# The low halves of a product's weights: GpSimd's subtraction tied by a semaphore to VectorE's row sums, and made two steps ahead

## The chip, the cores and the metric

The kernel runs on one core of a Trainium2 chip. The metric is the device time of one execution in microseconds (us); the profile is of one such execution on that core. Engine names are those of the profile: PE is TensorE (PEld its weight loads), DVE is VectorE, ACT is ScalarE, POOL is GpSimd, SP is SyncE, whose queue issues most loads.

## The reference, cut to what matters

Two transformer blocks run one after the other on 256 tokens of width 2048. The change lies in the last part of the second one, a layer of 16384 experts of which each token picks 128 (8 heads, 16 each):

```python
def peer_ffn(h, w_pq, sub_keys, u_tab, v_tab):
    ...
    expert = (e1 * N_KEYS + e2).reshape(T, PEER_HEADS * PEER_TOPK)
    gate = jax.nn.softmax(best, axis=-1).reshape(T, PEER_HEADS * PEER_TOPK).astype(h.dtype)
    def chunk(args):
        hc, ec, gc = args
        u = jnp.take(u_tab, ec, axis=0)
        act = jax.nn.gelu(jnp.einsum('cd,ckd->ck', hc, u), approximate=False) * gc
        vv = jnp.take(v_tab, ec, axis=0)
        return jnp.einsum('ck,ckd->cd', act, vv)
```

Its output is, for each token, a sum over its 128 picks of an activation times a row of `v_tab` (2048 wide).

## The kernel before, in words

Products are made in fp32r: a float32 operand is split into a high part (a copy rounded to fp32r) and a low part (the operand less its high part), and three matmuls (high by high, high by low, low by high) make one product.

The change lies in the second half of `_peer`, the output stage. Its result for 2 x 128 tokens lies in eight PSUM tiles `o` of 128x512: four column groups `g` for each token half `t`. The stage makes them in two ways:

- **By products, columns 0 to 1535.** The activations of all tokens for all 16384 experts lie in SBUF as `S_`, 128 slices of 128x256 (`sa` holds the first 52, `sb` the rest), zero where a token has not picked an expert. Step `e` of the loop at line 1582 multiplies slice `e` by 128 rows of `v`. It splits the slice into `ah` (ACT, line 1586) and `al` (POOL, line 1587), streams 1536 columns of `v` in three groups of 512 through `_stream`, and for each group issues, for both token halves, the matmuls (`ah`,`vh`), (`ah`,`vl`), (`al`,`vh`): 18 matmuls of 512 columns a step. The `v2` pool holds three `ah` and three `al`.
- **By rows, columns 1536 to 2047.** `_row_sums` fetches, for each of the 128 picks of every token, one row of 640 floats from the table `wide` in DRAM (512 columns of `v`, and the token's inner products with the expert). Row `j` takes two indirect DMAs from POOL's queue (line 1454), one a token half; ten row tiles `vrow` let them run four rows ahead. On DVE, one multiply a half (line 1468, a 128x128 product with the identity, summed along the row into the weight `w`) and one sum a half (line 1475: `o` plus row times weight, with `o` in PSUM) follow.

`_stream` (line 231) issues the loads of `v` on SP's queue: 1024 columns into a tile of `k.raw` (three of them) and 512 into a tile of `k.raw2` (six). For each 512 columns ACT copies `hi` (line 251) and DVE subtracts `lo` (line 254); there are four `hi` and four `lo`. In the trace these stand as `hi` and `lo` (`vh` and `vl` in the loop's words), and the matmuls as `o<-hi,ah`, `o<-lo,ah`, `o<-hi,al`, all at line 259.

The order on each engine is made by a scheduler that takes the program's order as priority. Line 1469 and line 1476 put each row's multiplies and sums behind the last `lo` on DVE, without a semaphore. The while loop at line 1598 takes one row in most steps and two in six of them, beginning at step 3.

Of the kernel before, what the change touches and what calls it, by code (L numbers as in the profile page):

```python
# [10 lines left out]
F32 = mybir.dt.float32  # L11
# [3 lines left out]
AF = mybir.ActivationFunctionType  # L15
OP = mybir.AluOpType
AX = mybir.AxisListType
NOSYNC = mybir.DependencyInfo(mybir.DependencyClass.NoSync, mybir.DependencyReason.DATA)

D = 2048  # L20
# [193 lines left out]
def _after(k, b, a):  # L214
    k.tc.add_manual_dep(b.ins, a.ins.name, NOSYNC, reason="one start per bank")

# [14 lines left out]
def _stream(k, src, total):  # L231
    nc = k.nc
    for r in range(0, total, k.rk * 256):
        n = min(total - r, k.rk * 256)
        if k.raw2 is not None and n <= 512:
            raw = k.raw2.tile([128, 512], F32, name="raw")
        else:
            raw = k.raw.tile([128, k.rk * 256], F32, name="raw")
        small = k.n == 0
        if not small:  # L240
            load = nc.sync.dma_start(raw[:, :n], src[:, r:r + n])
            if k.side:
                _after(k, nc.sync.dma_start(*k.side.pop(0)), load)
        step = 512 if small else k.gr
        for a in range(0, n, step):
            m = min(step, n - a)
            if small:
                nc.sync.dma_start(raw[:, a:a + m], src[:, r + a:r + a + m])
            hi = k.hi.tile([128, k.gr], F32R, name="hi")
            lo = k.lo.tile([128, k.gr], F32R, name="lo")  # L250
            nc.scalar.activation(hi[:, :m], raw[:, a:a + m], AF.Copy)  # L251
            k.n += 1
            eng = nc.gpsimd if k.pool_lo and k.n % k.pool_lo == 0 else nc.vector
            k.low = eng.tensor_tensor(lo[:, :m], raw[:, a:a + m], hi[:, :m].bitcast(F32), op=OP.subtract)  # L254
            yield hi, lo, m
# [96 lines left out]
def _first_mixer(k, I, rstd_n, rstd_b, mh, ml):  # L352
    nc, tc = k.nc, k.tc
    with ExitStack() as c:
# [207 lines left out]
        for pr in range(4):  # L562
# [9 lines left out]
            for hh in range(2):  # L572
# [4 lines left out]
                for t in range(2):  # L577
# [6 lines left out]
                    mx = at2.tile([128, 1], F32, name="mx")  # L584
                    nc.vector.tensor_reduce(mx, lg[:, :n], axis=AX.X, op=OP.max, negate=True)
                    sm = at2.tile([128, 1], F32, name="sm")
# [194 lines left out]
def _rwkv(k, I, rn, rb, y, qkv):  # L781
# [249 lines left out]
    def inverse(p, lq):  # L1031
# [5 lines left out]
        for t in range(1, 16):  # L1037
            nc.vector.tensor_tensor(tmp[:, :, 0:t], tt[:, :, 0:t], lq[:, 0:t, t][:, None, :].to_broadcast([128, 8, t]), op=OP.mult)  # L1038
            nc.vector.tensor_reduce(tt[:, :, t], tmp[:, :, 0:t + 1], axis=AX.X, op=OP.add)
        s2 = dram.tile([2, 4, 2, 4, 16, 16], F32, name="s2")  # L1040
# [64 lines left out]
    def chain(p, ars, pcs, am, dt, bon, gg, vz, bk):  # L1105
# [60 lines left out]
        mn = b2.tile([128, 4], F32, name="gm")  # L1166
        nc.vector.tensor_reduce(mn, y4, axis=AX.X, op=OP.add)
        nc.vector.tensor_scalar(mn, mn, 1.0 / 64, None, op0=OP.mult)
# [3 lines left out]
        vr = b2.tile([128, 4], F32, name="gv")  # L1172
        nc.vector.tensor_reduce(vr, sq2, axis=AX.X, op=OP.add)
        nc.vector.tensor_scalar(vr, vr, 1.0 / 64, 64e-5, op0=OP.mult, op1=OP.add)
# [60 lines left out]
def _gqa(k, y, qkv, g2, banks):  # L1235
# [17 lines left out]
    for m in range(8):  # L1253
# [11 lines left out]
        for h in range(2):  # L1265
# [9 lines left out]
            mx = g2.tile([128, 2], F32, name="gmx")  # L1275
            nc.vector.tensor_reduce(mx, sc, axis=AX.X, op=OP.max, negate=True)
            nc.vector.tensor_scalar(mx, mx, 0.125, None, op0=OP.mult)
# [51 lines left out]
class _Route:  # L1329
# [42 lines left out]
    def _pick(self, h, s):  # L1372
# [16 lines left out]
        for n in range(2):  # L1389
# [8 lines left out]
            for t in range(2):  # L1398
                nc.vector.tensor_tensor(eq[:, t], cf[:, t][:, :, None].to_broadcast([128, 16, 16]),
                                        self.iota[:, None, :].to_broadcast([128, 16, 16]), op=OP.is_equal)  # L1400
                nc.vector.tensor_tensor(eq[:, t], eq[:, t], fi[:, t, n][:, None, :].to_broadcast([128, 16, 16]), op=OP.mult)
            nc.vector.tensor_reduce(self.e[n][:, :, hs], eq, axis=AX.X, op=OP.add)

# [41 lines left out]
def _row_sums(k, picks, wide, rows, acc):  # L1445


    nc = k.nc
    ready = []

    def fetch(j):
        for t in range(2):
            r = rows.tile([128, DS + 128], F32, name="vrow")
            nc.gpsimd.indirect_dma_start(r, None, wide, bass.IndirectOffsetOnAxis(ap=picks.row[:, t, j:j + 1], axis=0),  # L1454
                                         element_offset=128 * t)
            ready.append(r)

    ahead = RB // 2 - 1
    for j in range(ahead):
        fetch(j)  # L1460
    for j in range(128):
        got = []
        for t in range(2):
            r = ready.pop(0)
            p, v = (r[:, DS:], r[:, :DS]) if t else (r[:, :128], r[:, 128:])

            w = picks.val[:, t, j:j + 1]
            i = nc.vector.scalar_tensor_tensor(p, p, picks.gate[:, t, j:j + 1], k.ident, op0=OP.mult, op1=OP.mult, accum_out=w)  # L1468
            _after(k, i, k.low)
            got.append((v, w))  # L1470
        for t, (v, w) in enumerate(got):
            if j == 0:
                i = nc.vector.tensor_scalar(acc[t], v, w, None, op0=OP.mult)
            else:
                i = nc.vector.scalar_tensor_tensor(acc[t], v, w, acc[t], op0=OP.mult, op1=OP.add)  # L1475
            _after(k, i, k.low)
        if j + ahead < 128:
            fetch(j + ahead)
        yield


def _peer(k, I, O, hctx, pers, sa, tctx, t1, x3n, wide, rb):
    nc, tc = k.nc, k.tc
# [20 lines left out]
    with ExitStack() as sctx:  # L1504
# [68 lines left out]

        with ExitStack() as c:
            pso = c.enter_context(tc.tile_pool(name="pso", bufs=1, space=bass.MemoryType.PSUM))
            v2 = c.enter_context(tc.tile_pool(name="v2", bufs=3, side="right"))
            k.raw2 = c.enter_context(tc.tile_pool(name="raw2", bufs=6, side="right"))
            out = [[pso.tile([128, 512], F32, name=f"o{t}{q}") for q in range(4)] for t in range(2)]
            rows = c.enter_context(tc.tile_pool(name="vr", bufs=RB, side="right"))
            sums = _row_sums(k, picks, wide, rows, [out[t][3] for t in range(2)])  # L1580
            taken = 0
            for e in range(128):
                src = S_[0][:, e] if e < SA else S_[1][:, e - SA]
                ah = v2.tile([128, 256], F32R, name="ah")
                al = v2.tile([128, 256], F32R, name="al")
                nc.scalar.activation(ah, src, AF.Copy)
                nc.gpsimd.tensor_tensor(al, src, ah.bitcast(F32), op=OP.subtract)  # L1587
                for g, (vh, vl, _) in enumerate(_stream(k, I["v"][e], D - DS)):
                    for t in range(2):
                        ts = slice(t * 128, t * 128 + 128)  # L1590
                        for n, (s_, m_) in enumerate(((ah, vh), (ah, vl), (al, vh))):
                            _mm(k, out[t][g], s_[:, ts], m_, start=e == 0 and n == 0, stop=e == 127 and n == 2)
                if e == 24:

                    xn = [S_[0][:, 8 * t:8 * t + 8].rearrange("p a b -> p (a b)").rearrange("p (a b) -> p a b", b=512) for t in range(2)]
                    for t in range(2):
                        nc.scalar.dma_start(xn[t], x3n[t].rearrange("p (a b) -> p a b", b=512))
                while taken < 128 and taken * 122 < (e - 2) * 128:
                    next(sums, None)
                    taken += 1  # L1600
            for _ in sums:
                pass
            k.raw2 = None
            sctx.close()
            fin = c.enter_context(tc.tile_pool(name="fin", bufs=1))
            nf = fin.tile([128, 4, 512], F32, name="nf")
            nc.scalar.dma_start(nf.rearrange("p a b -> p (a b)"), I["normf"].to_broadcast([128, D]))
            for t in range(2):
                ss = fin.tile([128, 4], F32, name=f"ss{t}")
                sq = fin.tile([128, 512], F32, name=f"fsq{t}")  # L1610
                for q in range(4):
                    nc.vector.tensor_tensor(xn[t][:, q], xn[t][:, q], out[t][q], op=OP.add)
                    nc.scalar.activation(sq, xn[t][:, q], AF.Square, accum_out=ss[:, q:q + 1])
                v = fin.tile([128, 1], F32, name=f"fv{t}")
                nc.vector.tensor_reduce(v, ss, axis=AX.X, op=OP.add)
                nc.vector.tensor_scalar(v, v, 1.0 / D, EPS, op0=OP.mult, op1=OP.add)
                r = _rsqrt(k, fin, v, 1, f"f{t}")
                for q in range(4):
                    nc.vector.scalar_tensor_tensor(xn[t][:, q], xn[t][:, q], r, nf[:, q], op0=OP.mult, op1=OP.mult)
                    (nc.sync if q % 2 else nc.scalar).dma_start(O["out"][t * 128:t * 128 + 128, q * 512:q * 512 + 512], xn[t][:, q])  # L1620
# [146 lines left out]
```

## Time and profile before

| | |
|---|---|
| median of 3 runs | 3388.03 us (3386.93 to 3388.34) |
| the profiled execution | 3391.95 us, its span 3390.1 us |
| PE busy over the span | 97% |
| DVE / ACT / POOL busy | 76% / 46% / 26% |
| mean granted clock of PE | 0.983 |
| HBM traffic over the span | 209 GB/s |

The page divides the span into 40 slices; the output stage fills the last seven, where DVE's digits are 9, PEld's 7 (against 9 before) and the DMA engines' 9. PE's busy time counts matmuls that overlap in the pipeline, so that a row of them with small pauses still reads as busy. How fast PE goes is read from the starts of its matmuls.

### The profile page before, as it was taken

The page shows a single profiled execution, that of the slowest core. Times are in us where ns is not written, and L with a number is a line of the kernel's source. Part 1 is how long each engine was busy: PE and PEld are TensorE (multiplying, and loading weights), DVE is VectorE, ACT ScalarE, POOL GpSimd, SP SyncE. Part 2 cuts the span into 40 slices and gives each one's busy share as a digit, 9 for nine tenths or more (in the row PEclk, how much of TensorE's full clock was granted, in tenths as well). Part 3 has the DMA queues.
Part 4 walks back from the last instruction along what each step waited for, and adds up shares of the span by engine and source line. Part 5 has one row for each costly group of instructions (what it writes and reads, how often), then busy time and mean ns, then how long its engine had stood idle before and what let it go on. Part 6 is the DMA issues. An engine that isn't in the chain of part 4 may idle for free.

```text
span 3390.1 us, 65776 instructions
## 1 busy us (share of the span) xinstructions
PE 3272.4 (97%) x25018; PEld 3050.2 (90%) x25018; DVE 2571.7 (76%) x5477; ACT 1572.2 (46%) x2810; POOL 866.4 (26%) x1036
## 2 busy tenths in 40 slices
PE   8999899999999979999999999999999999999998
PEld 8999899999999979888879999999999996777776
DVE  8775587777744468788865778776777869999999
ACT  5444444444433345555454544444444444444444
POOL 3110210000000055454410000001223226666663
PEclk9999999999999979999989999999999999999999
DMA  5545455555555568653126566666566679999996
GB/s 194 168 156 174 131 168 186 178 184 187 182 180 186 172 248 286 194 169 100 52 81 200 181 200 195 190 200 188 179 176 183 180 218 335 316 320 324 317 324 225
DMA packets 239341, 680.46 MB, mean 201 GB/s; under 512 B 58160, under 2 KB 88752, under 8 KB 214832
## 3 DMA queue, kind: packets, MB, share of 16 engines
q1 hardware_dynamic: 167824, 560.53, 51.0%
q0 software_dynamic: 20480, 83.90, 7.5%
q10 hardware_dynamic: 50720, 31.82, 3.2%
q8 instruction: 196, 3.21, 0.4%
q14 instruction: 121, 0.99, 0.1%
HBM read 649.55 MB, written 60.16 MB: 209 GB/s over the span
## 4 chain that ended last, share of the span: by engine, by line
PE 71%; DVE 17%; DMA 7%; issue 3%; ACT 1%; POOL 1%; SPq 0%; DVEq 0%; ACTq 0%; POOLq 0%
PE acc L259 57%; DVE lo L254 6%; PE held L259 5%; DMA raw<-in_v 4%; DVE vrow L1468 3%; DVE o L1475 2%; PE o L259 2%; PE ps_g L259 2%; PE R L259 1%; DVE hl L349 1%; DVE ltmp L1038 1%; PE ps_p L259 1%; DMA wide<-in_vs 1%; DMA s<-g 1%; PE ps_S L259 1%
## 5 line engine op out<-in xcount | busy, mean ns | idle before, releaser
L251 ACT ACTIVATE hi<-raw 128x512 fp32r<-128x512 f32 (+1 forms) x1582 | 1147.4, 732 | 1365.3 <-PE acc L259 864.7
L254 DVE TENSOR_TENSOR lo<-raw,hi 128x512 fp32r<-128x512 f32 (+1 forms) x1492 | 1229.1, 841 | 574.2 <-ACT hi L251 561.5
L259 PE MATMUL acc<-hh,hi 128*128 128x256 f32 x4928 | 1406.6, 286 | 22.2 <-ACT hh L348 13.4
L259 PE MATMUL acc<-hh,lo 128*128 128x256 f32 x4928 | 1407.1, 286 | 13.3 <-DVE lo L254 13.1
L259 PE MATMUL acc<-hl,hi 128*128 128x256 f32 x4928 | 1400.2, 284 | 7.5 <-DVE hl L349 7.4
L259 PEld LDWEIGHTS acc<-hh,hi 128*128 128x128 f32 x4928 | 938.4, 190 | 26.0 <-ACT hh L348 14.2
L259 PEld LDWEIGHTS acc<-hh,lo 128*128 128x128 f32 x4928 | 932.0, 189 | 18.6 <-DVE lo L254 16.8
L259 PEld LDWEIGHTS acc<-hl,hi 128*128 128x128 f32 x4928 | 938.1, 190 | 11.0 <-DVE hl L349 9.7
L259 PE MATMUL o<-lo,ah 128*128 128x512 f32 x768 | 314.4, 410 | 13.2 <-DVE lo L254 7.2
L1454 POOL DMA_INDIRECT vrow<-wide,prow x256 | 269.6, 1053 | 198.2 <-DVE o L1475 146.9
L259 PE MATMUL o<-hi,al 128*128 128x512 f32 x768 | 304.3, 398 | 5.4 <-POOL al L1587 5.4
L259 PE MATMUL o<-hi,ah 128*128 128x512 f32 x768 | 222.7, 399 | 9.3 <-ACT hi L251 8.3
L259 PEld LDWEIGHTS o<-lo,ah 128*128 128x128 f32 x768 | 144.6, 188 | 85.4 <-DVE lo L254 55.1
L259 PE MATMUL acc<-gh,lo 128*128 128x256 f32 x704 | 199.2, 283 | 0.0
L259 PE MATMUL acc<-gl,hi 128*128 128x256 f32 x704 | 199.2, 283 | 0.0
L259 PE MATMUL acc<-gh,hi 128*128 128x256 f32 x704 | 199.2, 283 | 0.0
L259 PEld LDWEIGHTS o<-hi,ah 128*128 128x128 f32 x768 | 143.7, 189 | 49.4 <-ACT hi L251 14.7
L1525 POOL TENSOR_SCALAR oh<-iota,sel 128x128 f32<-128x128 f32 x128 | 92.9, 736 | 352.7 <-PE ps_g L259 323.7
L259 PEld LDWEIGHTS o<-hi,al 128*128 128x128 f32 x768 | 145.8, 190 | 36.6 <-POOL al L1587 5.8
L1475 DVE SCALAR_TENSOR_TENSOR o<-vrow,pval,o 128x512 f32<-128x512 f32 x254 | 178.3, 744 | 0.0
L254 POOL TENSOR_TENSOR lo<-raw,hi 128x512 fp32r<-128x512 f32 (+1 forms) x90 | 132.4, 1473 | 157.5 <-ACT hi L251 144.7
L1468 DVE SCALAR_TENSOR_TENSOR vrow<-vrow,pgate,ident 128x128 f32<-128x128 f32 x256 | 163.8, 675 | 2.4 <-DMA vrow<-wide,prow 2.4
(476 smaller groups left out, 4320.4 us busy)
## 6 DMA issues: line engine op xcount, KB each, us to landing
raw<-in_u SPq DMA_DIRECT2D x256, 512.0 KB, 4.5
raw<-in_w_up SPq DMA_DIRECT2D x85, 1024.0 KB, 5.1
raw<-in_v SPq DMA_DIRECT2D x128, 512.0 KB, 5.9
raw<-in_w_in SPq DMA_DIRECT2D x43, 1024.0 KB, 5.1
raw<-in_w_dn SPq DMA_DIRECT2D x40, 1024.0 KB, 4.9
wide<-in_vs SPq DMA_DIRECT2D x64, 512.0 KB, 6.0
raw<-in_v SPq DMA_DIRECT2D x128, 256.0 KB, 6.0
raw<-in_w_rkv SPq DMA_DIRECT2D x48, 512.0 KB, 3.8
```

What stands on the lines that cost most here:

```text
L251: nc.scalar.activation(hi[:, :m], raw[:, a:a + m], AF.Copy)
L254: k.low = eng.tensor_tensor(lo[:, :m], raw[:, a:a + m], hi[:, :m].bitcast(F32), op=OP.subtract)
L259: return k.nc.tensor.matmul(out, lhsT, rhs, start=start, stop=stop, skip_group_check=True)
L349: k.nc.vector.scalar_tensor_tensor(lo, t, scale, hi.bitcast(F32), op0=OP.mult, op1=OP.subtract)
L1038: nc.vector.tensor_tensor(tmp[:, :, 0:t], tt[:, :, 0:t], lq[:, 0:t, t][:, None, :].to_broadcast([128, 8, t]), op=OP.mult)
L1454: nc.gpsimd.indirect_dma_start(r, None, wide, bass.IndirectOffsetOnAxis(ap=picks.row[:, t, j:j + 1], axis=0), element_offset=128 * t)
L1468: i = nc.vector.scalar_tensor_tensor(p, p, picks.gate[:, t, j:j + 1], k.ident, op0=OP.mult, op1=OP.mult, accum_out=w)
L1475: i = nc.vector.scalar_tensor_tensor(acc[t], v, w, acc[t], op0=OP.mult, op1=OP.add)
L1525: eng.tensor_scalar(aj, iota, sel[:, 0, t:t + 1], None, op0=OP.is_equal)
```

## The change

`ah` and `al` are made by a function `halves(e)`, called for steps 0 and 1 ahead of the loop and for step `e + 2` at the end of step `e`, behind the rows that this step takes. The last row multiply that was traced is kept as `k.own`, and from the first row on each subtraction on POOL waits for it by a semaphore. `v2` gets a fourth pair of tiles, `raw2` gives up one of its six.

```diff
+SYNC = mybir.DependencyInfo(mybir.DependencyClass.Sync, mybir.DependencyReason.DATA)
...
             i = nc.vector.scalar_tensor_tensor(p, p, picks.gate[:, t, j:j + 1], k.ident, op0=OP.mult, op1=OP.mult, accum_out=w)
             _after(k, i, k.low)
+            k.own = i
             got.append((v, w))
...
-            v2 = c.enter_context(tc.tile_pool(name="v2", bufs=3, side="right"))
-            k.raw2 = c.enter_context(tc.tile_pool(name="raw2", bufs=6, side="right"))
+            v2 = c.enter_context(tc.tile_pool(name="v2", bufs=4, side="right"))
+            k.raw2 = c.enter_context(tc.tile_pool(name="raw2", bufs=5, side="right"))
...
-            for e in range(128):
+            k.own, split = None, []
+            def halves(e):
                 src = S_[0][:, e] if e < SA else S_[1][:, e - SA]
                 ah = v2.tile([128, 256], F32R, name="ah")
                 al = v2.tile([128, 256], F32R, name="al")
                 nc.scalar.activation(ah, src, AF.Copy)
-                nc.gpsimd.tensor_tensor(al, src, ah.bitcast(F32), op=OP.subtract)
+                i = nc.gpsimd.tensor_tensor(al, src, ah.bitcast(F32), op=OP.subtract)
+                if k.own is not None:
+                    k.tc.add_manual_dep(i.ins, k.own.ins.name, SYNC, reason="beside the sums")
+                split.append((ah, al))
+            halves(0)
+            halves(1)
+            for e in range(128):
+                ah, al = split.pop(0)
                 for g, (vh, vl, _) in enumerate(_stream(k, I["v"][e], D - DS)):
...
                 while taken < 128 and taken * 122 < (e - 2) * 128:
                     next(sums, None)
                     taken += 1
+                if e < 126:
+                    halves(e + 2)
```

**POOL at the start of the stage.** The rows of the program before, from the first `al` on; `vrow<-wide` are the fetches of rows, `sb<-sb,gtmp` is the last piece of the stage ahead:

```order
L1587 TENSOR_TENSOR al<-sa,ah 128x256 x3
L1567 TENSOR_TENSOR sb<-sb,gtmp 128x512
L1454 DMA vrow<-wide,prow 128x640 x10
L1587 TENSOR_TENSOR al<-sa,ah 128x256 x3
L1454 DMA vrow<-wide,prow 128x640 x4
L1587 TENSOR_TENSOR al<-sa,ah 128x256
```

and of the changed program:

```order
L1593 TENSOR_TENSOR al<-sa,ah 128x256 x4
L1569 TENSOR_TENSOR sb<-sb,gtmp 128x512
L1455 DMA vrow<-wide,prow 128x640 x10
L1593 TENSOR_TENSOR al<-sa,ah 128x256
L1455 DMA vrow<-wide,prow 128x640 x2
L1593 TENSOR_TENSOR al<-sa,ah 128x256
```

The `al` of step 3 moves ahead of the first ten fetches; that of step 4 is now the first one behind them.

**POOL in the middle of the stage.** A step's rows on POOL with the semaphores that each waits for, before:

```order
L1454 DMA vrow<-wide,prow 128x640 [waits DMASW1_49,DVE_49]
L1587 TENSOR_TENSOR al<-sa,ah 128x256 [waits PE_49,Activation_49]
L1454 DMA vrow<-wide,prow 128x640 [waits DMASW2_49,DVE_49]
L1454 DMA vrow<-wide,prow 128x640 [waits DMASW3_49,DVE_49]
L1587 TENSOR_TENSOR al<-sa,ah 128x256 [waits PE_49,Activation_49]
```

and in the changed program:

```order
L1455 DMA vrow<-wide,prow 128x640 [waits DMASW1_49,DVE_49]
L1593 TENSOR_TENSOR al<-sa,ah 128x256 [waits DVE_49,PE_49,Activation_49]
L1455 DMA vrow<-wide,prow 128x640 [waits DMASW2_49,DVE_49]
L1455 DMA vrow<-wide,prow 128x640 [waits DMASW3_49,DVE_49]
L1593 TENSOR_TENSOR al<-sa,ah 128x256 [waits DVE_49,PE_49,Activation_49]
```

The order (two fetches, one `al`) stays; each `al` has a wait for DVE besides. Counted over the whole stage, `al` and `ah` of step `m` stand one step earlier against the fetches and against ACT's copies than before.

**ACT where two `ah` follow each other.** Some twelve steps into the stage before, then the first such place of the changed program, some ten steps in; `hi<-raw` are the copies of the streamed columns:

```order
L251 ACTIVATE hi<-raw 128x512 x3
L1586 ACTIVATE ah<-sa 128x256
L251 ACTIVATE hi<-raw 128x512 x3
L1586 ACTIVATE ah<-sa 128x256 x2
L251 ACTIVATE hi<-raw 128x512 x6
L1586 ACTIVATE ah<-sa 128x256 x2
L251 ACTIVATE hi<-raw 128x512 x6
L1586 ACTIVATE ah<-sa 128x256
```

```order
L252 ACTIVATE hi<-raw 128x512 x2
L1592 ACTIVATE ah<-sa 128x256
L252 ACTIVATE hi<-raw 128x512 x3
L1592 ACTIVATE ah<-sa 128x256 x2
L252 ACTIVATE hi<-raw 128x512 x6
L1592 ACTIVATE ah<-sa 128x256
L252 ACTIVATE hi<-raw 128x512 x3
```

Such places, with six `hi` behind two `ah`, stand in both programs: eight before, seven now. At the head of the stage four `ah` instead of three stand ahead of the first `hi`. On DVE the rows of the stage differ only around its first three rows, on PE the order differs where the first `al` stand, and the rest of the program is the same.

## Rows read from the trace of the kernel before

**Rows 1.** Instructions that write `o`: count, min/median/max ns, first and last start (us).
```profile
L259 PE MATMUL o<-hi,ah x768: 389/397/628, 2778.8 to 3374.2; 128*128 128x512 f32 x192
L259 PE MATMUL o<-hi,al x768: 390/397/793, 2780.7 to 3375.2; 128*128 128x512 f32 x192
L1475 DVE SCALAR_TENSOR_TENSOR o<-vrow,pval,o x254: 739/744/751, 2799.0 to 3362.7; 128x512 f32<-128x512 f32 x127
```

**Rows 2.** The chain of waits, last matmuls: start, us, what.
```profile
3346.75 26.97 PE o L259 x114
```

**Rows 3.** Busy time by stretch, instructions on `o` alone (x: how many).
```profile
2778.00:2800.00 22.00, 15.99 (x66) 12.19 (x66) 2.41 (x4) 1.00 0.94 321
2800.00:2820.00 20.00, 18.32 (x67) 14.63 (x68) 4.62 (x7) 0.83 0.88 294
2820.00:2860.00 40.00, 38.22 (x159) 28.62 (x158) 12.38 (x18) 1.00 0.97 354
2860.00:3360.00 500.00, 481.79 (x1951) 358.45 (x1950) 158.86 (x227) 1.00 0.92 316
3018.00:3054.00 36.00, 35.75 (x151) 27.89 (x150) 12.63 (x18) 1.00 0.94 330
```

**Rows 4.** The same for all instructions: PE, PEld, DVE, ACT, POOL, clock, DMA share, GB/s.
```profile
2860.00:3360.00 500.00, 481.79 (x1951) 358.45 (x1950) 496.89 (x1005) 237.71 (x434) 315.45 (x329) 1.00 0.92 316
```

**Rows 5.** Groups of instructions between 2860 and 3360 us.
```profile
L254 DVE TENSOR_TENSOR lo<-raw,hi 128x512 fp32r<-128x512 f32 x326 | 214.8, 708 | 3.1 <-ACT hi L251 3.1
L1468 DVE SCALAR_TENSOR_TENSOR vrow<-vrow,pgate,ident 128x128 f32<-128x128 f32 x226 | 148.9, 695 | 0.0
L1586 ACT ACTIVATE ah<-sb 128x256 fp32r<-128x256 f32 x75 | 31.4, 419 | 23.0 <-PE o L259 13.8
L1586 ACT ACTIVATE ah<-sa 128x256 fp32r<-128x256 f32 x34 | 14.2, 418 | 17.8 <-PE o L259 14.0
L1454 POOL DMA_INDIRECT vrow<-wide,prow x220 | 231.9, 1054 | 171.8 <-DVE o L1475 133.7 <-DVE lo L254 25.6 <-issue 6.3
```

**Rows 6.** Single lines, min/median/max ns: `lo` (2860 to 3360 us), multiplies, fetches, `al`.
```profile
L254 DVE TENSOR_TENSOR lo<-raw,hi x326: 674/678/1632, 2860.2 to 3359.3; 128x512 fp32r<-128x512 f32 x163
L1468 DVE SCALAR_TENSOR_TENSOR vrow<-vrow,pgate,ident x256: 335/344/1233, 2793.4 to 3361.1; 128x128 f32<-128x128 f32 x128
L1454 POOL DMA_INDIRECT vrow<-wide,prow x256: 943/962/1493, 2787.6 to 3342.4; - x128
L1587 POOL TENSOR_TENSOR al<-sb,ah x76: 737/748/1267, 3022.8 to 3363.7; 128x256 fp32r<-128x256 f32 x76
```

**Rows 7.** Timeline of POOL and DVE, a usual step.
```profile
3062.87 1.88 DVE L254 TENSOR_TENSOR lo<-raw,hi 128x512 fp32r<-128x512 f32 x3
3064.68 1.22 DVE L1468 SCALAR_TENSOR_TENSOR vrow<-vrow,pgate,ident 128x128 f32<-128x128 f32 x1
3065.00 0.74 POOL L1587 TENSOR_TENSOR al<-sb,ah 128x256 fp32r<-128x256 f32 x1
3067.43 0.68 DVE L254 TENSOR_TENSOR lo<-raw,hi 128x512 fp32r<-128x512 f32 x1
```

**Rows 8.** Timeline of DVE and POOL, a step with `al` behind the multiplies.
```profile
3041.75 1.88 DVE L254 TENSOR_TENSOR lo<-raw,hi 128x512 fp32r<-128x512 f32 x3
3043.83 0.34 DVE L1468 SCALAR_TENSOR_TENSOR vrow<-vrow,pgate,ident 128x128 f32<-128x128 f32 x1
3044.11 1.41 DVE L1475 SCALAR_TENSOR_TENSOR o<-vrow,pval,o 128x512 f32<-128x512 f32 x2
3044.55 0.75 POOL L1587 TENSOR_TENSOR al<-sb,ah 128x256 fp32r<-128x256 f32 x1
3045.45 1.49 POOL L1454 DMA_INDIRECT vrow<-wide,prow  x1 [0.16 <-issue]
3045.43 1.89 DVE L254 TENSOR_TENSOR lo<-raw,hi 128x512 fp32r<-128x512 f32 x3
```

**Rows 9.** Timeline of POOL and PE at the stage's start; `[...]` is the idle time ahead.
```profile
2799.92 0.95 POOL L1454 DMA_INDIRECT vrow<-wide,prow  x1 [0.30 <-DMA vrow<-wide,prow]
2801.68 1.22 PE L259 MATMUL o<-hi,al 128*128 128x512 f32 x2 [5.40 <-POOL al L1587]
```

**Rows 10.** Timeline of PE and ACT at places where two `ah` follow each other.
```profile
2864.04 0.39 PE L259 MATMUL o<-hi,al 128*128 128x512 f32 x1
2865.28 1.26 PE L259 MATMUL o<-hi,ah 128*128 128x512 f32 x4 [0.86 <-ACT hi L251]
2916.92 0.42 ACT L1586 ACTIVATE ah<-sa 128x256 fp32r<-128x256 f32 x1 [4.60 <-PE o L259]
```

**Rows 11.** DMA between 2860 and 3360 us: bytes of all queues.
```profile
DMA packets 48855, 158.14 MB, mean 316 GB/s; under 512 B 7005, under 2 KB 7005, under 8 KB 48816
```

## The prediction

> **What bounds the kernel now.** The page's 40 slices come first: only the last seven slices, the output stage, are touched by the change, and there three resources read nearly full at once: PE, DVE and the DMA engines. Which of them sets the pace has to be read from the stage itself.
>
> I begin with PE, as it has the least work that can be taken away. The stage's 2304 matmuls start between 2778.8 and 3375.2 us [rows 1], so 596.4 us for 2303 steps from start to start. What PE needs when nothing holds it is in the chain of waits: its last 114 matmuls took 26.97 us [rows 2], and with the 0.39 us of the last one itself taken off [rows 1] that is 26.58 / 113 = 0.2352 us from start to start. Then 2303 matmuls need 541.7 us, and **54.7 us of the stage are lost to waits**. The stretches show where [rows 3]: between 2860 and 3360 us 1951 matmuls need 458.9 of 500 us, so 41.1 us are lost there; the other 13.6 us nearly all at the start. A step of 18 matmuls needs 18 x 0.2352 = 4.23 us. There were 75 + 34 = 109 steps in the 500 us [rows 5], one in 4.587 us.
>
> Next, DVE: busy 496.9 of these 500 us [rows 4]. It sets the pace, and the groups show that part of its time is not work. The median multiply takes 0.344 us and the longest 1.233 [rows 6], and the mean between 2860 and 3360 us is 0.695 [rows 5]. The timeline shows when: in a usual step `al` runs on POOL beside the first multiply, which then takes 1.22 us [rows 7]. In the step of rows 8 `al` came behind the multiplies, beside the two sums: the multiply shown took 0.34 us, the sums 1.41 for both, `al` 0.75 as usual, and the step took 3045.43 - 3041.75 = 3.68 us. The 254 sums of the stage all lie between 739 and 751 ns [rows 1], so no sum was ever stretched, whatever POOL did. A `lo` can be stretched as the multiplies are (678 ns at the median, 1632 at most [rows 6]). The multiply and `lo` read two operands from SBUF, the sum one from SBUF and one from PSUM.
>
> So DVE gives to POOL 226 x (0.695 - 0.344) = 79.3 us in multiplies and 326 x (0.708 - 0.678) = 9.8 us in `lo` [rows 5, 6], 89.1 us or 0.82 us a step. Without them DVE needs (496.9 - 89.1) / 109 = 3.74 us a step, under PE's 4.23.
>
> **The change, part by part.** *The wait.* `al` of step m now waits on POOL until the second multiply of the row that DVE takes behind step m - 2's `lo` is done. It then starts with the two sums and needs 0.75 of their 1.41 us [rows 8]; DVE's 0.82 us a step come back. PE is then the bound, and the gain is not 0.82 but 4.587 - 4.23 = 0.36 us a step: the lost 41.1 us at most. Behind the waiting `al` on POOL stand the two fetches of the next row, which wait for the sums beside which `al` runs anyway, and rows are fetched four steps ahead. For `al` PE waits: it is needed when PE begins step m, a whole step (4.23 us) later at the least, and is done about 1.1 us behind its multiply (3044.55 + 0.75 against 3043.83 + 0.34 [rows 8]). I cost the wait at nothing.
>
> *Two steps ahead, four pairs of tiles.* `ah` moves one step forward on ACT, but with a fourth tile its wait for PE falls on the same matmul as before against the `hi` around it: nothing in a usual step. Where two `ah` follow each other, the second waits for PE (4.60 us [rows 10]) with the next `hi` behind it, PE runs dry, and its next matmul starts 2865.28 - 2864.04 = 1.24 us after the last instead of 0.235; the four behind it take 1.26 us, 0.17 more than at full pace [rows 10]. That is 1.2 us a place. There were eight and are now seven: **8.2 us that the change leaves standing**, one of them in the start.
>
> *A sixth `raw2` less.* The 512-column loads run further ahead than the 1024-column ones, whose three tiles stay. Bounds: nothing, or the rate rival below. I take nothing.
>
> *Rows taken two in a step.* Six steps have two more multiplies and sums, 2 x 0.34 + 1.41 less overlaps of some 0.2, so 1.9 us; DVE needs 5.6 us there, 1.4 over PE's step. DVE can lead by four `lo`. Bounds 0 and 6 x 1.4 = 8.4 us; nearer to zero, since the lead is built up at 0.5 us a step over 20 steps. I take 2 us, for these and stray loads.
>
> *The start.* PE stood idle 5.40 us until `al` of step 3, queued behind the ten fetches, was done at 2801.68 us [rows 9]; in the 20 us behind it 67 matmuls started where 85 fit, at a granted clock of 0.83 [rows 3]. Of these 18 x 0.2352 = 4.2 us, 1.7 are the idle time's end and 2.5 the clock, part of it at the lower of its two levels. Now step 3's `al` is ahead of the fetches, step 4's the first behind them. PE can go on for 14 matmuls more (its first `al` matmul stands eighth in step 4, twelfth in step 3 before), 3.3 us, and waits 2.1 instead of 5.40. Whether the clock still falls no row tells: 0 or 2.5 us. I take 0, as the idle time is less than half. Gain 3.3 + 2.5 = 5.8 us, and one pair of `ah` fewer, 1.2.
>
> **The sum.** Left over at the start: 13.6 - 5.8 - 1.2 = 6.6 us, with one pair in it; behind it six pairs, 7.2 us, and 2 us. Of 54.7 us 15.8 stay and **38.9 go**. From the profiled execution's 3391.95 us that leaves 3353.0; it stands 3.9 us over the median of the runs, so against 3388.03 the forecast is **3349 us**.
>
> **The rivals.** *The transfers become the bound.* A step moves 158.14 MB / 109 = 1.451 MB [rows 11]; at 4.23 us that is 343 GB/s, against 316 now at a busy share of 0.92 [rows 4]. For it: the share leaves 8%. Against it: 354 GB/s over 40 us, and in 36 us around the step of rows 8 PE made 151 matmuls, 0.238 us each, at 330 GB/s [rows 3]. Held at 330, a step takes 4.40 us: 109 x 0.19 = 20 us and the start's 5.8, so 3362 us.
>
> *The tie misses.* If POOL is still at its second fetch when the multiplies end, `al` slides behind the sums to the next `lo`, which waits as the multiply did, and DVE stays full. For it: in rows 8 `al` ended 0.2 us before the sums did. Against it: at PE's pace a step has 0.55 us more. Then only the start's gain is left: 3382 to 3388 us.
>
> *POOL becomes the bound, slower.* `al` no longer starts when POOL is free, so POOL's step is two fetches, `al` and their pauses: 2f + 0.75 + 0.30 + 0.16 [rows 8, 9]. With the mean fetch of 1.054 us [rows 5] this is 3.32 us; with the longest, 1.493 [rows 6], 4.20, just PE's step. Over f = 1.69 us POOL is slower than 4.587, and over about 1.72 the start's gain is used up too. At f = 2.0, a third over the longest seen, 5.21 us x 109 steps give 68 us more, less 5.8: 3450 us. Against it: fetches run beside `lo` already, as in rows 8, and will again. [...]
>
> **How the numbers follow.** The forecast has 0.76 (its own range 3339, with pairs and double rows free, to 3358, with the clock's 2.5 and double rows' 8.4 us not got back), the transfers 0.10, the missed tie 0.09, POOL 0.05. Faster by over 0.2% (6.8 us, what a measurement can tell) are the first two and the edge of the third, 0.88; the same 0.07; slower 0.05. The range runs from 3336, 3 us of scatter under the forecast's own end, to 3368, over the transfers' case.
>
> **What the changed profile would show.** Right: multiplies at a mean near 0.35 us and `lo` near 0.68; `al` released by DVE's multiply; DVE's busy share near 3.74 / 4.23 = 88%; the stage about 557 us long; DMA near 340 GB/s; pauses of about 1.2 us at the seven pairs. Wrong, if `lo` is stretched instead of the multiplies, if ACT waits for loads of `v` in most steps, if POOL shows no idle time, or if PE waits for `al` behind the start.

## The result and the profile after

The changed kernel takes **3346.26 us** (median of four runs, 3340.95 to 3347.91) against 3387.97 us before: a ratio of 0.9875 (95% interval 0.9858 to 0.9892), 41.7 us less. The forecast was 3349 us, its range 3336 to 3368. The profiled execution shown here took 3340.95 us, its span 3339.2 us.

The stage first. Instructions that write `o` (count, min/median/max ns, first and last start in us), to be laid beside [rows 1]:

```profile
L260 PE MATMUL o<-hi,ah x768: 389/397/608, 2770.6 to 3323.3; 128*128 128x512 f32 x192
L260 PE MATMUL o<-hi,al x768: 390/397/792, 2772.6 to 3324.2; 128*128 128x512 f32 x192
L1477 DVE SCALAR_TENSOR_TENSOR o<-vrow,pval,o x254: 740/750/759, 2791.0 to 3309.9; 128x512 f32<-128x512 f32 x127
```

The 2304 matmuls now start between 2770.6 and 3324.2 us: 553.6 us where it was 596.4, so the stage gives 42.8 us, and nothing else has to explain the 41.7 us of the medians. That it begins 8.2 us earlier than in the profile of before belongs to these two executions alone: the code ahead of it is the same, and over the profiles of this study it began anywhere from 2770.0 to 2781.3 us.

Its stretches, instructions on `o` alone, with the columns of [rows 3] (length, PE, PEld, DVE, clock, DMA share, GB/s):

```profile
2770.00:2792.00 22.00, 19.44 (x80) 14.74 (x80) 2.16 (x3) 1.00 0.96 323
2792.00:2812.00 20.00, 18.86 (x73) 14.49 (x73) 6.37 (x9) 0.91 0.95 337
2812.00:2852.00 40.00, 38.29 (x163) 29.95 (x162) 12.69 (x18) 1.00 1.03 400
2852.00:3310.00 458.00, 453.72 (x1932) 362.71 (x1931) 158.55 (x226) 1.00 0.95 340
```

In the long stretch 1932 matmuls fill 458 us, 0.2371 us each, where it was 500 / 1951 = 0.2563. At the pace of 0.2342 us that a run below shows free of waits they need 452.5 us, so 5.5 us of waiting are left there; another 5.8 lie in the stage's first 41.4 us, and most of the rest in two pauses between. Now the groups between 2852 and 3310 us, against [rows 5]:

```profile
L255 DVE TENSOR_TENSOR lo<-raw,hi 128x512 fp32r<-128x512 f32 x323 | 215.4, 702 | 42.1 <-issue 26.0 <-ACT hi L252 14.2 <-ACT ah L1592 1.8
L1469 DVE SCALAR_TENSOR_TENSOR vrow<-vrow,pgate,ident 128x128 f32<-128x128 f32 x226 | 69.5, 346 | 0.0
L1455 POOL DMA_INDIRECT vrow<-wide,prow x216 | 218.5, 1012 | 53.5 <-issue 37.1 <-DVE vrow L1469 5.5 <-DVE o L1477 0.9
L1593 POOL TENSOR_TENSOR al<-sb,ah 128x256 fp32r<-128x256 f32 x76 | 57.3, 754 | 76.8 <-DVE vrow L1469 73.1 <-issue 3.5
```

The mean multiply is back at 346 ns, from 695. The idle time ahead of `lo`, 3.1 us before, is now 42.1: DVE has time to spare. It is POOL that waits now: 73.1 of the 76.8 us that it stands idle ahead of these `al` are waits for the multiply, the new semaphore. The fetches wait for sums 0.9 us in all, where it was 133.7. The timeline shows a usual step, as [rows 7] did:

```profile
3102.74 0.69 DVE L255 TENSOR_TENSOR lo<-raw,hi 128x512 fp32r<-128x512 f32 x1 [0.46 <-issue]
3103.35 0.34 DVE L1469 SCALAR_TENSOR_TENSOR vrow<-vrow,pgate,ident 128x128 f32<-128x128 f32 x1
3103.62 0.35 DVE L1469 SCALAR_TENSOR_TENSOR vrow<-vrow,pgate,ident 128x128 f32<-128x128 f32 x1
3103.89 1.41 DVE L1477 SCALAR_TENSOR_TENSOR o<-vrow,pval,o 128x512 f32<-128x512 f32 x2
3104.14 0.74 POOL L1593 TENSOR_TENSOR al<-sb,ah 128x256 fp32r<-128x256 f32 x1 [1.05 <-DVE vrow L1469]
```

`al` lies inside the two sums, with 0.25 us to spare before it and 0.42 behind it, and costs them nothing. On DVE's and the DMA engines' side, all instructions of the same stretch (PE, PEld, DVE, ACT, POOL, clock, DMA share, GB/s):

```profile
2852.00:3310.00 458.00, 453.72 (x1932) 362.71 (x1931) 415.87 (x1001) 235.56 (x429) 300.68 (x325) 1.00 0.95 340
```

DVE is busy 415.87 of 458 us, 91% where it was 99, and the transfers run at 340 GB/s where it was 316. The bound is now PE. Behind the start its row of matmuls is broken only where two `ah` follow each other. One of these places, on ACT and PE, as [rows 10] showed:

```profile
2892.69 0.42 ACT L1592 ACTIVATE ah<-sa 128x256 fp32r<-128x256 f32 x1
2896.66 0.39 PE L260 MATMUL o<-hi,al 128*128 128x512 f32 x1
2896.91 0.42 ACT L1592 ACTIVATE ah<-sa 128x256 fp32r<-128x256 f32 x1 [3.80 <-PE o L260]
2897.90 1.25 PE L260 MATMUL o<-hi,ah 128*128 128x512 f32 x4 [0.86 <-ACT ah L1592]
```

The second `ah` stands 3.80 us in ACT's way, the `hi` behind it come late, and PE's next matmul starts 1.24 us after the last. This happens seven times (at 2814, 2849, 2897, 2982, 3072, 3157 and 3243 us), and at no other place behind the start.

### The profile page after: what moved, and what is told of

Its sections match the earlier page's. It is cut to its first block, busy times and chain, and to the rows that moved or that the text cites. A ratio compares the mean times of both kernels' runs of the same rounds, so it can differ in the third digit from the quotient of the medians.

```text
span 3339.2 us, 65782 instructions
## 1 busy us (share of the span) xinstructions
PE 3238.1 (97%) x25018; PEld 3049.6 (91%) x25018; DVE 2491.4 (75%) x5477; ACT 1571.5 (47%) x2810; POOL 854.9 (26%) x1036
## 4 chain that ended last, share of the span: by engine, by line
PE 83%; DVE 9%; DMA 3%; issue 2%; ACT 2%; POOL 1%; SPq 0%; ACTq 0%; DVEq 0%; POOLq 0%
PE acc L260 58%; PE o L260 13%; PE held L260 5%; DVE lo L255 2%; PE ps_g L260 2%; PE R L260 1%; DVE hl L350 1%; ACT hi L252 1%; DMA dst<-s 0%; PE ps_S L260 0%; DVE o L1477 0%; PE ps_m L260 0%; PE ps_p L260 0%; DVE x L677 0%; DVE ltmp L1039 0%
## 5 line engine op out<-in xcount | busy, mean ns | idle before, releaser
L260 PE MATMUL o<-lo,ah 128*128 128x512 f32 x768 | 305.0, 397 | 1.3 <-issue 1.3
L1455 POOL DMA_INDIRECT vrow<-wide,prow x256 | 259.6, 1014 | 67.9 <-issue 49.4
```

What stands on the lines that cost most here:

```text
L260: return k.nc.tensor.matmul(out, lhsT, rhs, start=start, stop=stop, skip_group_check=True)
```

## The experiments

Theory A in the expectations is that the tie alone gives the gain, by keeping `al` off the multiplies; theory B that it comes from making the halves two steps ahead. The runs were compared with the kernel before on their own chips (3388.48 us for the tie to the first multiply, the lead of three steps and the repeat, 3388.47 for the four others). All diffs are against the changed kernel.

**The lead without the tie.**

```diff
-                if k.own is not None:
-                    k.tc.add_manual_dep(i.ins, k.own.ins.name, SYNC, reason="beside the sums")
```

> The changed kernel without the semaphore: ah and al are still made two steps ahead with four pairs of tiles. Theory A (the tie is what gives time, because it moves al off VectorE's multiplies, which read two operands from SBUF, and beside the sums, which read one): al runs as soon as GpSimd's queue comes to it, beside the first multiply; VectorE's multiplies between 2860 and 3360 us again at a mean near 0.7 us, a step near 4.55 us, only the start's gain kept: 3376 to 3386 us. Theory B (the lead is what gives time, since PE and ScalarE no longer meet an unfinished pair): the same as with the tie, 3343 to 3350 us.

Measured: 3387.21 us, ratio 0.9997 (0.9987 to 1.0007): nothing is left of the gain, and the time lies a microsecond over the range of A. The groups and the stretch between 2860 and 3360 us read as before the change:

```profile
L1469 DVE SCALAR_TENSOR_TENSOR vrow<-vrow,pgate,ident 128x128 f32<-128x128 f32 x226 | 151.4, 706 | 0.0
...
2860.00:3360.00 500.00, 482.38 (x1948) 357.51 (x1947) 497.65 (x1005) 236.88 (x431) 308.28 (x324) 1.00 0.91 314
```

The multiplies are at 706 ns again and DVE is full, 497.65 of 500 us. B falls. Even what the earlier `al` saves at the start did not last: after the stage's first 41.4 us PE had started 17 matmuls more than before, 4 us ahead, and at its end, after 594.9 us, 1.5 us were left. DVE is the bound there, and what PE saves at the start it waits for DVE later.

**The tie with a lead of one step.** `halves(0)` alone stands ahead of the loop, the loop ends with `halves(e + 1)`, and the pools have their old sizes.

```diff
-            v2 = c.enter_context(tc.tile_pool(name="v2", bufs=4, side="right"))
-            k.raw2 = c.enter_context(tc.tile_pool(name="raw2", bufs=5, side="right"))
+            v2 = c.enter_context(tc.tile_pool(name="v2", bufs=3, side="right"))
+            k.raw2 = c.enter_context(tc.tile_pool(name="raw2", bufs=6, side="right"))
...
-            halves(1)
...
-                if e < 126:
-                    halves(e + 2)
+                if e < 127:
+                    halves(e + 1)
```

> The tie kept, the lead taken back to one step, with three pairs of tiles and six raw2 as before the change. Theory A: the tie alone gives nearly all; the start's wait of 5.4 us and its slower clock come back and there are eight places where two ah follow each other instead of seven, so 6 to 9 us slower than the changed kernel: 3350 to 3356 us, multiplies at a mean near 0.35 us. Theory B: without the lead the gain is lost, 3380 to 3390 us. Theory C (with the tie and no lead PE waits for al each step): over 3360 us, with waits of PE for al in most steps.

Measured: 3350.71 us, ratio 0.9893 (0.9877 to 0.991). The stage took 557.9 us, 4.3 more than with the lead of two. The multiplies stay short, and PE's waits (engine, waited for, us in total, times, longest) show the start's idle time back in one piece:

```profile
PE o L260 <- issue: 5.2, 1, 5.2
```

```profile
L1469 DVE SCALAR_TENSOR_TENSOR vrow<-vrow,pgate,ident 128x128 f32<-128x128 f32 x220 | 67.5, 345 | 0.0
```

So the tie carries some nine tenths of the gain and the lead some 4 us. Of these, 5.2 less the 2.2 us that PE waits in the changed kernel's start make 3.0, and an eighth pair of `ah`, whose pause the trace shows (2825 and 2834 us in place of the one at 2814), makes 1.2.

**The tie to the last `lo`, so that `al` meets the multiplies on purpose.**

```diff
-                    k.tc.add_manual_dep(i.ins, k.own.ins.name, SYNC, reason="beside the sums")
+                    k.tc.add_manual_dep(i.ins, k.low.ins.name, SYNC, reason="beside the multiplies")
```

> The same lead and pools as the changed kernel and as many waits, but al waits for the last subtraction lo of the step instead of for the second multiply of the row, so that it starts where the multiplies do. Theory A: the first multiply is stretched to about 1.2 us in nearly every step, VectorE needs about 4.55 us a step again, 3374 to 3388 us. Theory B, and the theory that any wait that spaces GpSimd's work would do: 3343 to 3350 us.

Measured: 3353.99 us, ratio 0.99 (0.9884 to 0.9917): neither theory's number. The timeline of a step and the group between 2860 and 3310 us say why:

```profile
3102.75 1.13 POOL L1455 DMA_INDIRECT vrow<-wide,prow  x1 [0.30 <-issue]
3103.59 0.34 DVE L1469 SCALAR_TENSOR_TENSOR vrow<-vrow,pgate,ident 128x128 f32<-128x128 f32 x1
3103.87 0.95 DVE L1469 SCALAR_TENSOR_TENSOR vrow<-vrow,pgate,ident 128x128 f32<-128x128 f32 x1
3103.91 0.75 POOL L1593 TENSOR_TENSOR al<-sb,ah 128x256 fp32r<-128x256 f32 x1
3104.75 1.40 DVE L1477 SCALAR_TENSOR_TENSOR o<-vrow,pval,o 128x512 f32<-128x512 f32 x2
```

```profile
L1469 DVE SCALAR_TENSOR_TENSOR vrow<-vrow,pgate,ident 128x128 f32<-128x128 f32 x216 | 120.2, 592 | 0.0
```

`al` does not begin at `lo`'s end (3103.67 us) but 0.24 us later, so it misses the first multiply and meets the second. What holds it is not the semaphore but the step's second fetch, which stands ahead of it on POOL and ends at 2.75 + 1.13 = 3103.88: between 2852 and 3310 us 98 of 105 `al` begin within 0.03 us of a fetch's end. Where the fetch was over early, `al` began 0.08 us behind `lo`'s end, here 2900.66 + 1.90 = 2902.56 us:

```profile
2902.64 0.79 POOL L1593 TENSOR_TENSOR al<-sa,ah 128x256 fp32r<-128x256 f32 x1 [1.82 <-DVE lo L255]
```

The second multiply of the step above is stretched by 0.61 us, not by the first one's 0.88 of [rows 7], since it begins nearly with `al` and not 0.32 us ahead of it. DVE then needs 3.68 + 0.61 = 4.29 us a step (4.28 in the trace), hardly over PE's 4.22: most of the gain survives by a hair. As expected, the multiply beside `al` is stretched until `al` is over (it ends 0.16 us behind, at 3104.82 against 3104.66); the expectation's price for one meeting was wrong, since it left out the fetch ahead of `al`.

**The tie to the first multiply instead of the second.**

```diff
-            k.own = i
+            if t == 0:
+                k.own = i
```

> The changed kernel with al tied to the first multiply of the row (token half 0) instead of the second. In the run that tied al to lo, al began 0.24 us behind the end of lo and stretched the second multiply by 0.61 us, to 0.16 us behind al's end. Theory A, with the stretch set by what VectorE is at when al begins: al begins about 0.24 us behind the first multiply's end, when the second is at its last tenth of a microsecond. If a multiply still needs what al holds that late (in the kernel before, al began 0.32 us behind a multiply's start and stretched it by 0.88 us), the second takes about 1.2 us, VectorE needs 4.55 us a step and the time is 3374 to 3386 us. If by then it has what it needs, al runs beside the sums and the time is the changed kernel's, 3341 to 3349 us.

Measured: 3347.63 us, ratio 0.9874 (0.9857 to 0.989), the changed kernel's time. In this kernel `al` stands at line 1594. Timeline of a step, and the group between 2860 and 3310 us:

```profile
3101.54 0.34 DVE L1469 SCALAR_TENSOR_TENSOR vrow<-vrow,pgate,ident 128x128 f32<-128x128 f32 x1
3101.81 0.35 DVE L1469 SCALAR_TENSOR_TENSOR vrow<-vrow,pgate,ident 128x128 f32<-128x128 f32 x1
3102.07 0.74 POOL L1594 TENSOR_TENSOR al<-sb,ah 128x256 fp32r<-128x256 f32 x1 [0.78 <-ACT hi L252]
```

```profile
L1469 DVE SCALAR_TENSOR_TENSOR vrow<-vrow,pgate,ident 128x128 f32<-128x128 f32 x220 | 67.7, 347 | 0.0
```

`al` begins 0.19 us after the first multiply's end (3101.88), where it is 0.17 us behind the second's in the step of the changed kernel. The profile puts the wait down to an ACT copy that ended last before it, but it is the tie: between 2852 and 3310 us 86 of 107 `al` begin 0.18 us behind the first multiply's end, as 85 of 109 begin 0.18 us behind the second's in the changed kernel. That delay brings `al` 0.26 us behind the start of the second multiply, which then keeps its 0.35 us although `al` begins before its end. So here the multiply, which starts first, runs through.

In two other kernels it does not, by the recorded starts. In the tie to `lo` the second multiply began 0.04 us ahead of `al` and was stretched to 0.95 us, and in the kernel before one that began 0.32 us ahead took 1.22 [rows 7]. In both, `al` follows the end of a fetch by 0.03 us. This is the fetch ahead of the `al` of [rows 7]:

```profile
3063.83 1.14 POOL L1454 DMA_INDIRECT vrow<-wide,prow  x1 [0.30 <-PE o L259]
```

`al` begins about as long behind the last `lo`'s end in both (0.25 us in the kernel before, 0.24 in the tie to `lo`), and yet it stretches the first multiply in the one and the second in the other. What differs is the semaphore: in the tie to `lo` it keeps `al` from being ready before `lo` ends, and in the kernel before `al` waited for nothing but the fetch. Whether that decides which multiply is stretched, no run tested by itself.

**`ah` behind the `hi` of its step on ACT.** In `_stream` the last `hi` is kept, and from step 6 on each `ah` is put behind it on ACT, as an order without a semaphore.

```diff
-            nc.scalar.activation(hi[:, :m], raw[:, a:a + m], AF.Copy)
+            k.high = nc.scalar.activation(hi[:, :m], raw[:, a:a + m], AF.Copy)
...
-                nc.scalar.activation(ah, src, AF.Copy)
+                h = nc.scalar.activation(ah, src, AF.Copy)
+                if e > 5:
+                    _after(k, h, k.high)
```

> The changed kernel with an order edge (no semaphore) that keeps each ah from step 6 on behind the three copies hi of the step two ahead of it on ScalarE, so that no two ah follow each other. If the pauses of PE of 1.25 us at seven places come from a second ah that waits for PE with hi queued behind it, they go, 7 x 1.2 = 8.4 us: 3336 to 3340 us, and all steps behind the start take 4.22 us. If they come from the steps with two rows (VectorE late), they stay: 3344 to 3349 us.

Measured: **3334.18 us**, ratio 0.9847 (0.983 to 0.9863), the fastest of the study and 12 us under the changed kernel, where 6 to 10 were expected. The stage took 546.2 us, 7.4 less; the rest of the 12 us is no more than the runs of one kernel differ by. The long stretch, instructions on `o` alone and then all:

```profile
2852.00:3310.00 458.00, 458.00 (x1956) 368.18 (x1956) 159.06 (x227) 1.00 0.95 344
...
2852.00:3310.00 458.00, 458.00 (x1956) 368.18 (x1956) 419.37 (x1002) 239.32 (x435) 301.31 (x324) 1.00 0.95 344
```

PE never stops: 458 of 458 us, 24 matmuls more than the changed kernel in the same time. All seven pauses are gone, which shows that they came from the order on ACT. PE's own pace can be read here without any wait in it, 458 / 1956 = 0.2342 us a matmul or 4.22 us a step. And the transfers keep up with it at 344 GB/s.

**A lead of three steps on top of that**, with five pairs of tiles in `v2` and four tiles in `raw2`.

```diff
-            v2 = c.enter_context(tc.tile_pool(name="v2", bufs=4, side="right"))
-            k.raw2 = c.enter_context(tc.tile_pool(name="raw2", bufs=5, side="right"))
+            v2 = c.enter_context(tc.tile_pool(name="v2", bufs=5, side="right"))
+            k.raw2 = c.enter_context(tc.tile_pool(name="raw2", bufs=4, side="right"))
...
+            halves(2)
...
-                if e < 126:
-                    halves(e + 2)
+                if e < 125:
+                    halves(e + 3)
```

> The version with the order edge on ScalarE, and the lead taken to three steps: five pairs of tiles, four raw2. Step 4's al then stands ahead of the first fetches on GpSimd too, and only seven fetches ahead of step 5's. If the start's wait for al is what is left of the start's loss, 2 to 4 us go: 3330 to 3333 us on the median. If the start is held by the first rows' landing or by loads of v (two raw2 fewer than before the change), it is the same as with the order edge alone, 3333 to 3337 us.

Measured: 3337.84 us, ratio 0.9849 (0.9832 to 0.9865): no gain over the lead of two that these runs can tell. The stage took 544.7 us, 1.5 less. PE no longer waits for `al` at the start: in the stage's first 41.4 us it started 160 matmuls where it was 149, 2.6 us ahead, but after 80 us only 6 matmuls were left of that. ACT waits for loads of `v` in these 80 us, but no more than with the lead of two. The lead of three (2776 to 2852 us), then the lead of two (2771 to 2847):

```profile
ACT hi L252 <- DMA raw<-in_v: 17.4, 9, 3.4
```

```profile
ACT hi L252 <- DMA raw<-in_v: 17.6, 8, 3.7
```

So these loads can hold both kernels there, but they are not a price of the third step or of the fewer tiles. What took the rest of the 2.6 us, no run shows.

**The changed kernel once more**, for the scatter of the stage.

> The changed kernel itself, unchanged, on the chip of these runs, as the measure for the two others: 3341 to 3349 us. Its stage from the first product into o to the last takes 553 to 555 us again; what differs from run to run lies ahead of it.

Measured: 3346.38 us, ratio 0.9871 (0.9855 to 0.9888), with a stage of 554.7 us (2776.4 to 3331.1) against 553.6. So a microsecond in the stage is within what two profiles differ by, and the 4.3, 7.4 and 42.8 us above are not.

## Why the prediction was right, step by step

**DVE gives time to POOL, and the tie gives it back: right.** The multiplies fell from 695 to 346 ns, the first experiment put them back by taking the tie alone away, and the kernel's time followed both times. This was the step with nearly all of the money in it. `lo` was the small miss in it: 702 ns at the mean, not 678. Every `lo` is a little longer (the median is 686 ns), and some are still stretched (1225 at most); why, no run shows. That is 323 x 0.024 = 7.8 us, more than half of what makes DVE busy 91% and not 88.

**PE becomes the bound: right.** The forecast took the pace from the chain's last 114 matmuls, 0.2352 us (they begin right behind a wait and end at 3373.72 us [rows 2], ahead of the stage's last); it is 0.2342 (4.22 us a step, not 4.23). Over 2303 matmuls that is 2.3 us, the largest part of the 3.9 us by which the stage gave more than the forecast's 38.9.

**The new wait costs nothing: right.** POOL waits for the multiply in most steps, and what is queued behind it, the fetches, come in time: DVE's multiplies show no idle time at all in the long stretch, and PE waits there for `hi` and `ah` alone.

**Pairs of `ah`, 1.2 us each at seven places: right in size and number.** Two of the seven lie in the first 80 us, where the forecast put one.

**Steps with two rows, 2 us: too much.** In the changed kernel all steps behind the start take 4.22 us but for the seven pauses; DVE's lead covered them whole. Where DVE has no room, they cost: with the tie to `lo` PE's step took 5.3 us at four of the five such places behind the start.

**The start: right in sum, not in its parts.** In the first 41.4 us 152 matmuls started, which need 35.6 us at 0.2342; 5.8 us are lost, and the forecast left 6.6 less one pair, 5.4. But it had a single wait of 2.1 us for `al` and no fall of the clock. The timeline of DVE, PE and POOL:

```profile
2788.85 1.41 DVE L1475 TENSOR_SCALAR o<-vrow,pval 128x512 f32<-128x512 f32 x2
2790.16 0.68 DVE L255 TENSOR_TENSOR lo<-raw,hi 128x512 fp32r<-128x512 f32 x1
2790.90 0.73 PE L260 MATMUL o<-lo,ah 128*128 128x512 f32 x2 [1.33 <-issue]
2791.69 1.27 POOL L1593 TENSOR_TENSOR al<-sa,ah 128x256 fp32r<-128x256 f32 x1
2793.01 1.22 PE L260 MATMUL o<-hi,al 128*128 128x512 f32 x2 [0.91 <-issue]
2794.03 0.63 PE L260 MATMUL o<-lo,ah 128*128 128x512 f32 x1
2794.45 0.63 PE L260 MATMUL o<-hi,al 128*128 128x512 f32 x1
...
2796.41 0.39 PE L260 MATMUL o<-lo,ah 128*128 128x512 f32 x1
2796.64 0.39 PE L260 MATMUL o<-hi,al 128*128 128x512 f32 x1
```

Only the second of the two waits, 0.91 us, ends with `al` of step 4 (2791.69 + 1.27 = 2792.96). The first, 1.33 us, ends with a `lo` (2790.16 + 0.68 = 2790.84) that stood on DVE behind the first row's sums. And the clock did fall: some three microseconds of matmuls start 0.43 us apart instead of 0.23, at a granted clock of 0.50 (2793 to 2796 us), the same as in the kernel before from 2801 to 2807 us (1.00 from 2808 to 2811). The fall that the forecast priced at nothing was paid, and the `al` that it priced at 2.1 us took less. That the two misses cancel is luck, and they do so in this profile: in the second one of the same kernel `al` is waited for 2.41 us in one piece, and the first 41.4 us lose 7.0.

**The rivals.** *The transfers as the bound* was to hold the rate at 330 GB/s; the changed kernel moved 340, and with PE never waiting 344. *The missed tie* did not come about: the sums outlast `al` by 0.42 us. *POOL as the bound*: the 256 fetches beside DVE took 1.56 us at most and 1.01 at the mean, under the 1.69 from which that rival decided, and POOL stood idle a third of the stretch.

## What to carry to other kernels

When an engine reads as full, compare the mean of each of its instructions with the shortest of the same shape before looking for work to take off it; here a sixth of DVE's time, 79.3 of 496.9 us, was one small instruction stretched by another engine's, to 695 ns at the mean from 344. Such a meeting can be moved instead of removed, by tying the other engine's instruction to the start of work that it does not disturb, if what waits behind it has room. And once the bound has moved, look at the order on the engines that feed the new one: fixing two copies on ACT was worth another 7 us. Before, with DVE as the bound, it should have been worth nothing, though no run tried it there.

## What the runs showed of the hardware

- **The price of a meeting depends on who comes when.** A 128x128 multiply on DVE with two SBUF operands took 0.34 us alone, 0.95 when it began 0.04 us ahead of `al`, 1.22 in the kernel before, and 0.35 when `al` came 0.26 us after its start behind a semaphore. The stretched ones end 0.16 us after `al` (3103.87 + 0.95 against 3103.91 + 0.75; 3064.68 + 1.22 against 3065.00 + 0.74 in [rows 7]). The 254 sums, with one operand in PSUM, took 740 to 759 ns in the changed kernel with `al` beside some nine tenths of them, and 739 to 751 before with `al` beside one in ten.
- **A semaphore's delay is long enough to matter here.** From the recorded end of the multiply on DVE to the start of `al` on POOL it was 0.18 us, in 85 `al` of the changed kernel and 86 of the tie to the first multiply; from `lo`'s end, where no fetch stood between, 0.08 us (2902.56 to 2902.64). In the tie to the first multiply it brought `al` behind the start of the second one, which then ran through.
- **Around PE's short waits the granted clock read from 0.66 to 1.00.** In the second profile of the changed kernel PE waited 2.41 us in one piece, and the 10 us from 2796 us on, which hold it, ran at a granted clock of 0.66; in the first it waited 1.33 and 0.91 us with matmuls between, and the 20 us from 2792 us on had 0.91; with `ah` behind `hi` it waited twice, 1.08 and 1.04 us, and the 10 us from 2792 us on kept 1.00. The first and the last of these stretches, all instructions; the second changed profile, then the kernel with `ah` behind `hi`:

```profile
2796.00:2806.00 10.00, 7.59 (x21) 5.66 (x21) 8.05 (x20) 2.89 (x5) 8.71 (x9) 0.66 0.99 360
```

```profile
2792.00:2802.00 10.00, 7.81 (x31) 5.58 (x32) 8.47 (x19) 4.98 (x10) 8.87 (x9) 1.00 0.94 338
```

  PE was busy for about as long in both, 7.59 and 7.81 us, and started 21 matmuls in the one and 31 in the other.
- **Transfers.** Over 40 us the DMA engines moved 400 GB/s (2812 to 2852 us of the changed kernel), more than any stretch of 10 us or longer of before that was read (388 at most).
